# Hybrid encoder: a granule of the Fourier output weights split earlier, and a half tile's transposing DMA moved behind the next product

## The chip, the cores and the metric

The kernel runs on one core of one Trainium2 chip. The metric is the device time of the whole program in microseconds (us), as the median of several runs. Lower is better.

## The reference

Two layers of three residual steps each, and a final RMSNorm, on 512 tokens of 1024 channels in float32:

```python
x = x + 0.5 * swiglu(rms_norm(x, g1), w_in1, w_out1)          # d_ff 2816
z = rms_norm(x, gm) @ mix_w_in                                # q, k, v, u, two gates
y_na = neighbourhood_attention(q, k, v, rpb) @ w_na_out       # 8 heads of 64, 8x64 grid
y_f = fft2(u, axes=(tokens, channels of a group)).real @ w_f_out
x = x + (sigmoid(ga + b0) * y_na + sigmoid(gf + b1) * y_f) @ w_o
x = x + 0.5 * swiglu(rms_norm(x, g2), w_in2, w_out2)
```

## The kernel before

**Arithmetic.** Products are made of three passes of a 12-bit-rounded high part and the remainder: for every weight granule (128 partitions by 1024 columns, 512 KB) ScalarE writes the rounded high part `whi` (line 191) and VectorE the low part `wlo` (line 194), and TensorE runs high by high, high by low and low by high (lines 502 to 505 in the large products, 316 to 318 in the others). The large products are done by a seven-product Strassen scheme, in the order 1, 5, 6, 2, 7, 3, 4 in the feed-forward stages. TensorE gets its work in this order, block after block.

**The weight stream.** A list of items, one per granule, is written out ahead in the order of use. `next` hands the next granule out and first splits two more (`AHEAD = 2`); every split of the item with number p first loads items up to number p + 7 (`FETCH = 8`):

```python
def fetch(self, to):                       # line 280
    while self.loaded < min(to, n) and ...: self.items[self.loaded].load(); ...
def prep(self, to):                        # line 286
    while self.prepped < min(to, n) and ...:
        self.fetch(self.prepped + self.depth)
        self.items[self.prepped].prep(...)
```

A load is a plain DMA on SP's queue (line 148). For two of the four quadrants of a block's weights, c and d, a second DMA on GpSimd's queue (line 150) then adds a into c and c into d in SBUF; these are the accumulating loads. A `Raw` object has `t` set to None until its load is traced. The raw buffers are nine, so most loads on SP wait for the `wlo` of an older granule.

**Feed-forward stage** (`stage_ffn`, four times). Five blocks, of fourteen items each, two for each of the seven products; in three of the stages the first block (`first_block`) has 21 items and half a block more. Items 2 and 3 of a block are d, items 8 and 9 are c (the first granule of a block has number 0). At the end of a block the gated result of the second half of the tokens, `z2`, is put through `halves`: `apart` (line 342) splits its 32-bit words into 16-bit halves with two ScalarE copies into `zs` and lets a transposing DMA on SP's queue (line 348) write `zt`. Then comes product 4, the last of the block, and then the same for `z1`. In the next block ScalarE joins the halves again (`joined`, line 357, `at<-zt`). After the last block of a stage it joins z1 first.

ScalarE, VectorE and SP's queue are ordered by the scheduler here, which simulates the program and takes what is ready, lines higher up first. Instructions of one engine run in the order in which the scheduler put them.

**Mixer** (`stage_mixer`, twice). Here the order on ScalarE, VectorE and TensorE is the order of the code. The part around lines 1577 to 1611: the Fourier branch's low parts `yf` (line 1247), the scores of attention steps 2 and 3 (`p2`, `p3`: row maxima at line 1295, exponentials at 1304, reciprocals at 1307, scaling at 1312), the key projection `k3` on TensorE, then `rows_of(yf, 0, first_f)`, the Fourier branch's output product, which needs two weight granules. `ws.prep(ws.pos + 1)` at 1585 splits the first of them, `ws.prep(ws.pos + 2)` at 1593 the second.

Of the kernel before, what the change touches and what calls it, by code (L numbers as in the profile page):

```python
# [9 lines left out]
F32 = mybir.dt.float32  # L10
# [3 lines left out]
U16 = mybir.dt.uint16  # L14
# [4 lines left out]
P = 128  # L19
# [72 lines left out]
def encoder_kernel(  # L92
    ctx: ExitStack, tc: tile.TileContext, xin, xtr, wst, gains, gfin, gbias, bias_in, dft, chan, ident_in, rot, out
):
    nc = tc.nc
# [12 lines left out]
    def nm(s):  # L108
        uid[0] += 1
        return f"{s}_{uid[0]}"  # L110

    def slot(dt=F32, s="k", shape=(4, 256)):
        return kp.tile([P, *shape], dt, tag="k", name=nm(s), bufs=23)
# [38 lines left out]
    class Item:  # L152
# [26 lines left out]
        def prep(self, nxt):  # L179
# [16 lines left out]
                G.dma_start(out=t, in_=wst[GRAN_AT[self.then]][:, 0:n], accum_op=ALU.add)  # L196
            self.out = (hi, lo)

    def stage_items():
        items, st = [], 0  # L200

        def add(*a, **k):
            items.append(Item(*a, stage=st, **k))

        def strassen(s, name, idx, sizes, order, dma=False, behind=None):
            def key(q, g):
                return (s, name(q), idx, g) if g < 2 else (s, "h" + q, idx, 0)

            r = {}
            for q, q2 in (("a", None), ("b", None), ("c", "a"), ("d", "c")):  # L210
                r[q] = [Raw(key(q, g), n, q2 and key(q2, g)) for g, n in enumerate(sizes)]
            d2 = [Raw(key("d", g), n) for g, n in enumerate(sizes)]
            at = [(m, g) for m in order for g in range(len(sizes))]
            if len(sizes) == 3:
                at.remove((2, 2))
                at.insert(at.index((7, 2)), (2, 2))
            for m, g in at:
                a, b, c, d = [r[q][g] for q in "abcd"]
                if m == 1:
                    add(a, neg=True)  # L220
                elif m == 2:
                    add(b)
                elif m == 3:
                    add(d, None if dma else b)
                elif m == 4:
                    add(d2[g])
                elif m == 5:
                    add(d)
                elif m == 6:
                    add(d, a, then=b.key if dma else None)  # L230
                else:
                    add(c)
                for key in (behind or {}).get(m, ()) if g == len(sizes) - 1 else ():
                    add(Raw(key))

        def out_sizes(c):
            return (1024, 512) if c == 0 else (1024, 1024)

        def ffn(s):
            first = not items  # L240
            if first:
                for g in range(4):
                    add(Raw((s, "cl", g)), parts=2 if g < 2 else 1, pieces=2 if g == 0 else 1)
            for j in range(NB):
                order = (1, 2, 5, 6, 7, 3, 4) if first and j == 0 else (1, 5, 6, 2, 7, 3, 4)
                strassen(s, lambda q: q, j, (1024,) * (2 if first or j else 3), order)
            for order in ((1,), (2,), (5, 6, 7, 3), (4,)):
                for c in range(3):
                    summed = s == (L - 1, 2) and c == 2
                    strassen(s, lambda q: "o" + q, c, out_sizes(c), order, summed)  # L250

        for l in range(L):
            ffn((l, 1))
            st += 1
            s = (l, 0)
            two = (1024, 1024)
            qk = [(s, "qk", g) for g in range(8)]
            strassen(s, lambda q: "u" + q, 0, two, (1, 5, 6, 2, 3, 7, 4), True, behind={5: qk[0:1], 6: qk[1:2], 2: qk[2:3], 3: qk[3:4], 7: qk[4:5]})
            for key in qk[5:] + [(s, "f", g) for g in range(4)]:
                add(Raw(key))  # L260
            st += 1
            for g in range(2):
                add(Raw((s, "n", 0, g)))
            st += 1
            for i in range(2):
                strassen(s, lambda q: "g" + q, i, two, ORDER, True)
            for g in range(2):
                add(Raw((s, "n", 1, g)))
            strassen(s, lambda q: "w" + q, 0, two, ORDER, True)
            ffn((l, 2))  # L270
        return items
# [40 lines left out]
    ws = Stream()  # L312
# [26 lines left out]
            V.scalar_tensor_tensor(r, t, 1.5, r, ALU.add, ALU.mult)  # L339
        return r  # L340

    def apart(z):

        s, t = slot(U16, "zs", (2, 4, 2, P)), slot(U16, "zt", (2, 4, 256))
        words = z.bitcast(U16).rearrange("p b (q f h) -> p h q b f", q=4, h=2)
        for h in range(2):
            S.activation(s[:, h], words[:, h], AF.Copy)  # L347
        nc.sync.dma_start_transpose(
            out=t.rearrange("p h q (b t) -> p (h q b) t", b=2), in_=s.rearrange("p h q b f -> p (h q b f)")
        )  # L350
        return t

    def joined_words(to, t):

# [254 lines left out]
    def stage_ffn(norm, nxt, late):  # L609

        hx, lx = norm.h, norm.l
        at = {}

        def at_tile(h, j, c):
# [72 lines left out]
        def halves(z, j, f0):  # L687

            turned.append((apart(z), j, f0))

        def joined():

# [35 lines left out]
        def times(z, u, j):  # L728
            for b in range(2):
                c = 2 * j + b  # L730
                V.scalar_tensor_tensor(z[:, b, :], u[b], norm.r2[:, c : c + 1], z[:, b, :], ALU.mult, ALU.mult)  # L731
# [68 lines left out]
        def first_block():  # L800

            f0 = 2

            def snap_T(ps):
                t = slot(F32, "sn", (2, 256))
                S.activation(t, ps.rearrange("p (m t) -> p m t", m=2), AF.Copy)
                return t

            def less_T(ps, t):
                V.tensor_tensor(t, ps.rearrange("p (m t) -> p m t", m=2), t, ALU.subtract)  # L810

            pa, ha = pair("A"), bank("hA")
            product(pa, acts[1], K4, True)
            combine(5)
            s1 = snap(pa)
            if len(norm.due) == 2:
                norm.quad(*norm.due.pop(0))
            product_T(ha, acts[1], True)
            h1 = snap_T(ha)
            pb, hb = pair("B"), bank("hB")  # L820
            product(pb, acts[5], K4, True)
            combine(6)
            sb = snap(pb)
            norm.settle()
            product_T(hb, acts[5], True)
            hsb = snap_T(hb)
            norm.rstd()
            norm.spread(R)
            product(pa, acts[6], K4, False, again=True)
            s2 = snap(pa)  # L830
            combine(7)
            product_T(ha, acts[6], False)
            h2 = snap_T(ha)
            pc = pair("C")
            product(pc, acts[2], K4, True)
            less(pc, s1)
            combine(4)
            z1 = gate(s1, 0)
            product(pa, acts[7], K4, False, again=True)
            hc = bank("hC")  # L840
            product_T(hc, acts[2], True)
            less_T(hc, h1)
            r1 = half_gate(h1, 0)
            less(pa, sb)
            product_T(ha, acts[7], False)
            less_T(ha, hsb)
            product(pb, acts[3], K4, False, again=True)
            less(pb, s2)
            z2 = gate(s2, 1)
            times(z2, [sb[:, 0, :], sb[:, 1, :]], 1)  # L850
            product_T(hb, acts[3], False)
            less_T(hb, h2)
            r2 = half_gate(h2, 1)
            half_times(h2, r2, hsb, hsb, 1)
            halves(z2, 1, f0)
            product(pa, acts[4], K4, False, again=True)
            times(z1, pa, 0)
            halves(z1, 0, f0)
            product_T(ha, acts[4], False)
            half_times(h1, r1, ha.rearrange("p (m t) -> p m t", m=2), h2, 0)  # L860
# [4 lines left out]
        for jb in range(0 if first else 1, NB):  # L865
# [35 lines left out]
                make(1)  # L901
            z2 = gate(s2, 1)
            times(z2, [sb[:, 0, :], sb[:, 1, :]], 1)
            halves(z2, 1, f0)
            if jb == NB - 1:
                make(2)
            product(pa, acts[4], K4, False, again=True)
            times(z1, pa, 0)
            halves(z1, 0, f0)

# [137 lines left out]
    def stage_mixer(l, norm, nxt):  # L1048
# [427 lines left out]
        yf = []  # L1476
# [24 lines left out]
        with tc.manual_schedule(engines={mybir.EngineType.DVE, mybir.EngineType.Activation}):  # L1501
            with tc.manual_schedule(engines={mybir.EngineType.PE}):
# [77 lines left out]
                q3 = q3()  # L1580
                p2, p3 = [Probs(i, att_scores(i)) for i in (2, 3)]
                k3 = proj_T(None, 0)
                p2.maxes(0)
                p2.maxes(1)
                ws.prep(ws.pos + 1)
                p2.exps(0)
                p2.exps(1)
                p3.maxes(0)
                p2.inverse(0)
                p3.maxes(1)  # L1590
                p2.inverse(1)
                yf += [w0(), w1()]
                ws.prep(ws.pos + 2)
                p2.scaled(0)
                p2.scaled(1)
                p3.exps(0)
                k[2] = k2()
                p3.inverse(0)
                p3.exps(1)
# [394 lines left out]
```

## Time and profile before

| | |
|---|---|
| median of 3 runs | 1852.29 us (1851.4, 1852.29, 1854.55) |
| the profiled execution | 1856.7 us |
| its span, first to last instruction | 1854.9 us |
| busy in it: TensorE / VectorE / ScalarE / GpSimd | 1838.5 / 1601.6 / 1312.2 / 173.1 us |
| mean granted TensorE clock | 0.998 |
| mean DMA rate | 213 GB/s |

Rows of a timeline read: start in us, duration in us, engine, line, operation, tiles written <- read, shape, count of merged instructions, and in brackets the engine's idle time ahead of it and what ended it. PE is TensorE, DVE VectorE, ACT ScalarE, POOL GpSimd; SPq is SyncE, all of whose instructions issue DMAs: an instruction there lasts from its start on the queue, with its wait, until it has been issued.

### The profile page before, as it was taken

Reading aid. Unit: us, or ns where it says so; the run is one execution under the profiler, and the core shown is the slowest. Engines: PE = TensorE matmul, PEld = TensorE weight load, DVE = VectorE, ACT = ScalarE, POOL = GpSimd, SP = SyncE. Lnnn points to the kernel's source line nnn. Section 1 sums busy time; section 2 is a strip of 40 time slices with the busy share of each in tenths; the row PEclk is TensorE's granted clock in tenths of the full one; section 3 lists DMA queues with packets and bytes.
Section 4 is the critical chain, followed back from the end, with each engine's and each line's share of the span. In section 5 each row is a group of like instructions: output and inputs, shape, how many; then the busy total and the mean of one; then the engine's idle time right before and its main releaser. Section 6 shows DMA issues by size and latency. Waiting matters only on the chain.

```text
span 1854.9 us, 24564 instructions
## 1 busy us (share of the span) xinstructions
PE 1838.5 (99%) x8850; PEld 1530.0 (82%) x8850; DVE 1601.6 (86%) x1942; ACT 1312.2 (71%) x1777; POOL 173.1 (9%) x212
## 2 busy tenths in 40 slices
PE   9999999999999999999999999999999999999998
PEld 7888888888888888888888888888888888788886
DVE  7878899786989987889998888998869899787898
ACT  6777875668576777777667778665776776677865
POOL 0001010100111010001010100101001111010010
PEclk9999999999999999999999999999999999999999
DMA  9898799934887798979888887988258866989795
GB/s 297 229 231 223 189 275 272 232 103 126 236 234 173 180 221 228 211 198 270 248 197 225 222 218 198 284 288 187 85 181 201 227 174 184 201 225 218 214 282 148
DMA packets 198282, 395.72 MB, mean 213 GB/s; under 512 B 103760, under 2 KB 103888, under 8 KB 198160
## 3 DMA queue, kind: packets, MB, share of 16 engines
q1 hardware_dynamic: 168912, 294.23, 50.4%
q0 software_dynamic: 28816, 99.38, 30.2%
q8 instruction: 69, 1.13, 0.2%
q10 hardware_dynamic: 432, 0.55, 0.1%
q14 instruction: 53, 0.43, 0.1%
HBM read 367.88 MB, written 2.11 MB: 199 GB/s over the span
## 4 chain that ended last, share of the span: by engine, by line
PE 88%; DVE 4%; ACT 3%; DMA 2%; issue 1%; SPq 0%; ACTq 0%; DVEq 0%
PE A L505 9%; PE A L502 9%; PE A L503 9%; PE o L505 7%; PE o L502 7%; PE o L503 7%; PE B L503 5%; PE B L502 5%; PE B L505 5%; PE C L502 2%; PE C L503 2%; PE C L505 2%; PE ps L316 2%; PE ps L317 2%; PE ps L318 2%; DMA zt<-zs 2%
## 5 line engine op out<-in xcount | busy, mean ns | idle before, releaser
L194 DVE TENSOR_TENSOR wlo<-raw,whi 128x1024 fp32r<-128x1024 f32 (+1 forms) x534 | 630.0, 1189 | 183.9 <-ACT whi L191 180.0
L191 ACT ACTIVATE whi<-raw 128x1024 fp32r<-128x1024 f32 (+1 forms) x534 | 545.4, 1033 | 253.4 <-DVE raw L164 53.2
L150 POOL DMA_DIRECT2D raw<-in_wst_dram x166 | 144.3, 889 | 1361.0 <-DMA raw<-in_wst_dram 532.1
L164 DVE TENSOR_TENSOR raw<-raw,raw 128x1024 f32<-128x1024 f32 (+1 forms) x148 | 175.9, 1189 | 2.0
L503 PE MATMUL A<-whi,xl 128*128 128x512 f32 x400 | 155.7, 389 | 0.0
L502 PE MATMUL A<-whi,xh 128*128 128x512 f32 x400 | 155.7, 389 | 0.0
L357 ACT ACTIVATE at<-zt 128x1024 uint16<-128x1024 uint16 (+2 forms) x96 | 110.2, 1166 | 22.9 <-DMA zt<-zs 22.9
L186 ACT ACTIVATE whi<-raw 128x1024 fp32r<-128x1024 f32 (+1 forms) x83 | 85.9, 1037 | 44.0 <-issue 12.5
L505 PE MATMUL A<-wlo,xh 128*128 128x512 f32 x400 | 115.0, 389 | 0.0
L187 DVE SCALAR_TENSOR_TENSOR wlo<-raw,whi 128x1024 fp32r<-128x1024 f32 (+1 forms) x83 | 98.2, 1191 | 12.7 <-ACT whi L186 12.7
L505 PEld LDWEIGHTS A<-wlo,xh 128*128 128x128 f32 x400 | 75.1, 188 | 15.5
L503 PEld LDWEIGHTS A<-whi,xl 128*128 128x128 f32 x400 | 75.1, 188 | 15.4
L502 PEld LDWEIGHTS A<-whi,xh 128*128 128x128 f32 x400 | 75.1, 188 | 15.4
L502 PE MATMUL C<-whi,xh 128*128 128x512 f32 x208 | 81.1, 390 | 0.1
L503 PE MATMUL C<-whi,xl 128*128 128x512 f32 x208 | 81.0, 389 | 0.0
L502 PE MATMUL B<-whi,xh 128*128 128x512 f32 x208 | 81.0, 389 | 0.0
L503 PE MATMUL B<-whi,xl 128*128 128x512 f32 x208 | 81.0, 389 | 0.0
L724 ACT ACTIVATE th<-sn,rh 128x512 f32<-128x512 f32 x80 | 55.1, 716 | 36.1 <-DVE sn L577 35.2
L347 ACT ACTIVATE zs<-th 128x1024 uint16<-128x1024 uint16 x80 | 79.5, 1042 | 1.3 <-DVE th L731 1.3
L572 ACT ACTIVATE sn<-A 128x512 f32<-128x512 f32 x104 | 59.0, 583 | 23.6 <-PE A L505 23.6
L505 PE MATMUL C<-wlo,xh 128*128 128x512 f32 x208 | 59.8, 389 | 0.0
L505 PE MATMUL B<-wlo,xh 128*128 128x512 f32 x208 | 59.8, 389 | 0.0
(428 smaller groups left out, 4678.8 us busy)
## 6 DMA issues: line engine op xcount, KB each, us to landing
raw<-in_wst_dram SPq DMA_DIRECT2D x468, 512.0 KB, 5.9
raw<-in_wst_dram POOLq DMA_DIRECT2D x176, 512.0 KB, 7.9
bm<-in_bias_dram SPq DMA_DIRECT2D x16, 512.0 KB, 4.4
raw<-in_wst_dram SPq DMA_DIRECT2D x30, 256.0 KB, 4.5
x<-in_xin_dram SPq DMA_DIRECT2D x4, 512.0 KB, 10.2
raw<-in_wst_dram POOLq DMA_DIRECT2D x8, 256.0 KB, 8.6
dft<-in_dft_dram POOLq DMA_DIRECT2D x8, 256.0 KB, 11.0
gb<-in_gbias_dram SPq DMA_DIRECT2D x4, 512.0 KB, 9.1
```

The costliest lines, as they stand in the source:

```text
L150: G.dma_start(out=self.t, in_=wst[GRAN_AT[self.plus]][:, 0 : self.n], accum_op=ALU.add)
L164: V.tensor_tensor(self.raw.t, self.raw.t, self.add.t, ALU.add)
L186: S.activation(hi, t, AF.Copy, scale=-1.0)
L187: self.last = V.scalar_tensor_tensor(lo, t, -1.0, hi.bitcast(F32), ALU.mult, ALU.subtract)
L191: S.activation(hi[:, cs], t[:, cs], AF.Copy)
L194: self.last = V.tensor_tensor(lo[:, cs], t[:, cs], hi[:, cs].bitcast(F32), ALU.subtract)
L347: S.activation(s[:, h], words[:, h], AF.Copy)
L357: S.activation(to[:, w], t[:, w], AF.Copy)
L502: PE.matmul(ps, lh, rh, start=start, stop=False, skip_group_check=again)
L503: PE.matmul(ps, ll, rh, start=False, stop=False, skip_group_check=again)
L505: PE.matmul(ps, lh, rl, start=False, stop=stop, skip_group_check=again)
L572: S.activation(t[:, b, :], ps[b], AF.Copy)
```

## The change

Two edits.

In the mixer, the four VectorE instructions of `w0()` and `w1()` go ahead of p2's maxima; the second granule's high part (ScalarE) goes ahead of p2's exponentials, its low part (VectorE) behind p2's reciprocals; and the second pair of p3's maxima goes behind the granule's low part and behind p3's first exponentials.

In the feed-forward stages, `apart` is cut in two. The ScalarE copies of z2 stay where they were. Its transposing DMA is written behind product 4, inside `behind_sums`: where the accumulating load of granule 1 of quadrant c of the next block has been traced, a DMA of 64 bytes out of that granule's buffer is issued on SP, and the transposing DMA is queued behind it; where that load has not been traced (`raw.t is None`) or there is no next block, nothing is added.

```diff
@@ strassen
+                sums.update({z.key: z for z in r[q] if z.plus})
@@ apart
-    def apart(z):
-        s, t = slot(U16, "zs", (2, 4, 2, P)), slot(U16, "zt", (2, 4, 256))
+    def words_apart(z):
+        s = slot(U16, "zs", (2, 4, 2, P))
...
+    def turned_words(s):
+        t = slot(U16, "zt", (2, 4, 256))
         nc.sync.dma_start_transpose(
...
+    def apart(z):
+        return turned_words(words_apart(z))
@@ stage_ffn
+        stage = (norm.idx // 3, 1 + (norm.idx % 3) // 2)
...
+        def behind_sums(jb):
+            raw = sums.get((stage, "c", jb, 1))
+            if raw is None or raw.t is None:
+                return nullcontext()
+            seen = dp.tile([16], F32, tag="seen", name=nm("seen"))
+            to = bass.AP(tensor=seen.tensor, offset=seen.offset, ap=[[16, 1], [1, 16]])
+            return tc.issue_after(nc.sync.dma_start(out=to, in_=raw.t[0:1, 0:16]))
@@ first_block (the other blocks alike, with jb + 1)
-            halves(z2, 1, f0)
+            z2 = words_apart(z2)
             product(pa, acts[4], K4, False, again=True)
+            with behind_sums(1):
+                turned.append((turned_words(z2), 1, f0))
             times(z1, pa, 0)
             halves(z1, 0, f0)
@@ stage_mixer
                 k3 = proj_T(None, 0)
+                yf += [w0(), w1()]
                 p2.maxes(0)
                 p2.maxes(1)
                 ws.prep(ws.pos + 1)
+                low = ws.prep_high()
                 p2.exps(0)
                 p2.exps(1)
+                p2.inverse(0)
                 p3.maxes(0)
-                p2.inverse(0)
-                p3.maxes(1)
                 p2.inverse(1)
-                yf += [w0(), w1()]
-                ws.prep(ws.pos + 2)
+                low()
                 p2.scaled(0)
                 p2.scaled(1)
                 p3.exps(0)
+                p3.maxes(1)
                 k[2] = k2()
```

More of the change, by code (lines that the diff above doesn't have):

```diff
@@ L197, in prep @@
             self.out = (hi, lo)
+    sums = {}
     def stage_items():
@@ L347, in apart @@
             S.activation(s[:, h], words[:, h], AF.Copy)
+        return s
+    def turned_words(s):
+        t = slot(U16, "zt", (2, 4, 256))
         nc.sync.dma_start_transpose(
@@ L903, in stage_ffn @@
             times(z2, [sb[:, 0, :], sb[:, 1, :]], 1)
-            halves(z2, 1, f0)
+            z2 = words_apart(z2)
             if jb == NB - 1:
@@ L907, in stage_ffn @@
             product(pa, acts[4], K4, False, again=True)
+            with behind_sums(jb + 1):
+                turned.append((turned_words(z2), 1, f0))
             times(z1, pa, 0)
```

## The prediction

> **What bounds the kernel now.** I read the page first, then what TensorE waits for, then the timelines around the two waits that the edits touch.
>
> ```profile
> span 1854.9 us, 24564 instructions
> PE 1838.5 (99%) x8850; PEld 1530.0 (82%) x8850; DVE 1601.6 (86%) x1942; ACT 1312.2 (71%) x1777; POOL 173.1 (9%) x212
> PE 88%; DVE 4%; ACT 3%; DMA 2%; issue 1%; SPq 0%; ACTq 0%; DVEq 0%
> ```
>
> TensorE is busy for all but 1854.9 − 1838.5 = 16.4 us, the start and the end of the program included. Neither edit removes a matmul, so a gain can only come out of these 16 us. The view of TensorE's own waits names two that matter inside the program:
>
> ```profile
> PE A L502 <- ACT whi L191: 2.7, 1, 2.7
> PE ps L317 <- DVE wlo L194: 2.1, 2, 1.0
> ```
>
> The second is the Fourier output product waiting for its second weight granule, once in each mixer; the first edit is about it. The first is one long wait, in which a transposing DMA has a part; the second edit bears on that. A time within 0.2% of 1852.29 us, that is within 3.7 us, is about what a measurement of this kernel can tell from no change.
>
> **The mixer edit.** TensorE's timeline in the two mixers:
>
> ```profile
> 425.00 0.39 PE L317 MATMUL ps<-wlo,y 128*128 128x512 f32 x1
> ...
> 425.91 0.39 PE L318 MATMUL ps<-whi,y 128*128 128x512 f32 x1
> 426.14 0.39 PE L316 MATMUL ps<-whi,y 128*128 128x512 f32 x1
> 427.56 0.50 PE L317 MATMUL ps<-wlo,y 128*128 128x512 f32 x1 [1.04 <-DVE wlo L194]
> ...
> 1344.28 0.39 PE L316 MATMUL ps<-whi,y 128*128 128x512 f32 x1
> 1345.69 0.50 PE L317 MATMUL ps<-wlo,y 128*128 128x512 f32 x1 [1.03 <-DVE wlo L194]
> ```
>
> Matmuls of this shape start 426.14 − 425.91 = 0.23 us apart. The step at the wait is 427.56 − 426.14 = 1.42 us in the first mixer and 1345.69 − 1344.28 = 1.41 in the second, so each wait costs 1.42 − 0.23 = 1.19 us and the two together 2.4 us. That is all there is to gain here. Whether it is gained depends on when VectorE ends the low part in the new order. The old order:
>
> ```profile
> 419.46 0.41 DVE L1295 CUSTOM_DVE_ANT_0 s<-ps,bm 128x256 f32<-128x256 f32 x1
> ...
> 421.52 1.23 DVE L194 TENSOR_TENSOR wlo<-raw,whi 128x1024 fp32r<-128x1024 f32 x1 [0.60 <-ACT whi L191]
> 422.66 0.42 DVE L1295 CUSTOM_DVE_ANT_0 s<-ps,bm 128x256 f32<-128x256 f32 x1
> ...
> 423.35 0.16 DVE L1307 RECIPROCAL rs<-sm 128x2 f32<-128x2 f32 x1
> 423.42 0.40 DVE L1295 CUSTOM_DVE_ANT_0 s<-ps,bm 128x256 f32<-128x256 f32 x1
> ...
> 424.17 2.20 DVE L1247 TENSOR_TENSOR y<-fy,y 128x256 fp32r<-128x256 f32 x4
> 426.30 1.21 DVE L194 TENSOR_TENSOR wlo<-raw,whi 128x1024 fp32r<-128x1024 f32 x1
> ```
>
> From start to start, the four low parts y take 426.30 − 424.17 = 2.13 us, a pair of maxima 423.35 − 422.66 = 0.69, a reciprocal 0.07, a granule's low part 422.66 − 421.52 = 1.14. In the new order the y go first: 419.46 to 421.59. Two pairs of p2's maxima: to 422.97. First granule's low part: to 424.11, complete 1.23 after its start, at 424.20; TensorE wants it at 425.00, so this delay of 1.45 us is covered with 0.8 us to spare. Reciprocal, one pair of p3's maxima, reciprocal: 0.83, to 424.94. Second granule's low part: complete 1.21 later, at 426.15. TensorE heard of the old one 427.56 − (426.30 + 1.21) = 0.05 after its end, so here at 426.20, and wants it at 426.14 + 0.23 = 426.37. The wait goes, with 0.17 us to spare. ScalarE must not be later than that:
>
> ```profile
> 420.41 1.07 ACT L191 ACTIVATE whi<-raw 128x1024 fp32r<-128x1024 f32 x1
> 421.36 0.52 ACT L1304 ACTIVATE s<-s,nmx 128x256 f32<-128x256 f32 x1
> ...
> 423.33 1.06 ACT L191 ACTIVATE whi<-raw 128x1024 fp32r<-128x1024 f32 x1
> 424.28 1.71 ACT L1312 ACTIVATE s<-s,rs 128x256 f32<-128x256 f32 x4
> ```
>
> The second high part moves to 421.36 and takes 0.95, so p2's exponentials run from 422.31 for 423.33 − 421.36 = 1.97 us, to 424.28. Their first maxima are there at 422.3, the second reciprocal asks for the last sum at 424.87, 0.6 us after it is written, and the scaling starts at 424.28 as before. The moved pair of p3's maxima ends at about 424.94 + 1.14 + 0.69 = 426.8, when the exponentials that need it are due on ScalarE. No load moves with the granule: the Fourier granules are the last of the stream's stage, and all four are fetched before this point. TensorE then runs 1.19 us earlier into products that follow it one for one. The gain is between 0 (the low part 1.2 us later than worked out, all spare time wrong) and 2.4 us for both mixers; I take 2.4, since every term has its own row and the sum leaves something over.
>
> **The transposing DMA.** The first question is whether the tiny transfer is issued at all. The lookup wants granule 1 of quadrant c of the next block, item 9 of that block. Product 4 takes the last two items of a block. The last `next` splits item 1 of the next block, and that split has loaded items up to 1 + 7 = 8, which is granule 0 of c. In the first block of 21 items one more granule of the block is still to come, and the loads reach item 7. So at each of the 20 places `raw.t` is None or there is no next block, and nothing is added: no transfer, no wait, no forced order. I cost it at nothing; nobody queues behind it.
>
> What is left is that the transposing DMA of z2 is written behind product 4 rather than ahead of it, so behind the two granule loads that this product issues on SP. GpSimd's queue holds none of the moved work; its accumulating load for granule 0 of c still waits for the plain load. Does the DMA's place on SP's queue change? SP's order is not the code's:
>
> ```profile
> 986.31 7.92 SPq L348 DMA_TRANSPOSE zt<-zs  x2
> 994.33 5.46 SPq L148 DMA_DIRECT2D raw<-in_wst_dram  x3
> ```
>
> This is a first block: both transposing DMAs, z2's and z1's, stand ahead of the loads, though z1's is written behind product 4's two loads even now. The loads have no free buffer at that time, and the scheduler takes what is ready. With z2's DMA written just ahead of z1's, it is ready as early as before and the loads no earlier, so I expect the same order there and in the other blocks, and a cost between −1 and +1 us; I take 0.
>
> That leaves the long wait, in the first block of the last stage:
>
> ```profile
> 1582.82 0.86 POOL L150 DMA_DIRECT2D raw<-in_wst_dram  x1 [10.35 <-DMA raw<-in_wst_dram]
> 1583.97 0.85 POOL L150 DMA_DIRECT2D raw<-in_wst_dram  x1 [0.29 <-DVE at L798]
> ...
> 1584.03 19.88 SPq L348 DMA_TRANSPOSE zt<-zs  x2
> ...
> DMA to landing us min/median/max: 4.3/5.7/20.2
> ...
> 1604.29 1.36 ACT L357 ACTIVATE at<-zt 128x1024 uint16<-128x1024 uint16 x1 [4.92 <-DMA zt<-zs]
> ...
> 1608.27 0.50 PE L502 MATMUL A<-whi,t7h 128*128 128x512 f32 x1 [2.73 <-ACT whi L191]
> 1613.18 0.39 PE L502 MATMUL A<-whi,t7h 128*128 128x512 f32 x1
> ...
> 1608.50:1613.50 5.00, 5.00 (x16) 3.91 (x16) 5.00 (x6) 3.87 (x5) 0.81 (x1) 0.66 0.98 364
> ```
>
> An accumulating load was issued 0.06 us before the transposing DMA started. The two then held each other up: 20.2 us to landing against a median of 5.7. ScalarE stood still for 4.92 us before `at<-zt`, the weight split behind it was late, and TensorE waited 2.73 us. The 14 matmul steps from 1608.27 to 1613.18 then took 4.91 us instead of 14 × 0.23 = 3.2, at a granted clock of 0.66. The event cost 2.7 + 1.7 = 4.4 us. It is one of three such first blocks; the other two show nothing on TensorE. The accumulating load in it is the one for d of the next block, not the c that the edit names.
>
> The Trainium skill, DMA: Bandwidth & Descriptors, Rules for kernel authors, says that a transpose next to ordinary DMAs needs nothing; the 20.2 us row speaks against that as far as time goes, if an accumulating load counts as ordinary, and by the rule no reordering on SP could win anything. TensorE: Matmul & The Clock Gate, What's actually happening, has the clock fall after an idle window of about 3.4 us; here it fell after 2.73, and by the rule the event would have cost 2.7 us, not 4.4.
>
> **The sum.** The profiled execution took 1856.7 us, 1.8 more than its span. Less the 2.4 of the mixers it gives 1854.3 if the long wait comes again. The median of the runs, 1852.29, is 4.4 under the profiled one, just what the long wait cost, so I read the median as a time without it: 1852.29 − 2.4 = 1849.9 us, 0.13% faster.
>
> **Rivals.**
>
> Forecast, chance 0.46: the mixers' waits go, SP's order stays, 1849.9. Its own range is 1848.3 to 1852, from the gain's end at zero and from the runs' distance from their median; 0.10 of the 0.46 lies under 1848.6.
>
> The transposing DMA comes free of the accumulating load, 0.24. Written later, z2's DMA goes out some us after the load that it met, and the long wait is absent from the timed runs. For it: the event hangs on 0.06 us, and the slowest of the three runs is 2.3 above the median, so part of it may be in them. Against: nothing forces the order. Full price 1852.29 − 2.4 − 4.4 = 1845.5.
>
> The mixer edit brings nothing, 0.10: the low part meets a wait that the sum does not show (a maximum waiting for TensorE, a late exponential), eating the 0.17 us to spare and 1.2 more. 1852.3, within 0.2%.
>
> Slower, 0.20: SP does follow the code. In the last block of each stage z1 is joined first, and its DMA lands just in time:
>
> ```profile
> 821.03 3.54 SPq L348 DMA_TRANSPOSE zt<-zs  x1
> 824.67 1.01 SPq L148 DMA_DIRECT2D raw<-in_wst_dram  x2
> 827.03 2.90 SPq L348 DMA_TRANSPOSE zt<-zs  x1
> ...
> 833.76 2.58 ACT L357 ACTIVATE at<-zt 128x1024 uint16<-128x1024 uint16 x2 [3.60 <-DMA zt<-zs]
> ```
>
> With the two loads ahead, z2's DMA would start at 824.67 + 1.01 = 825.7 and hold SP for 3.54, to 829.2, so z1's starts 2.2 us later than at 827.03. ScalarE is already standing there, so TensorE pays most of 2.2, in four stages 8.8: 1852.29 − 2.4 + 8.8 = 1858.7. It decides from the point where z2's DMA stands behind both loads there. Against: the first-block rows. I put 0.16 over 1856.0 and 0.04 under.
>
> **How the numbers follow.** Faster by over 0.2%: 0.10 + 0.24 = 0.34. Within: 0.36 + 0.10 + 0.04 = 0.50. Slower: 0.16. The range leaves out the slower case's upper part and little else: from the second case's full price, 1845.5, to 1854.5, the profiled sum with the long wait in it.
>
> **What would show it.** Right: no wait of line 317 for `wlo` in either mixer, and the second granule's low part about 0.2 us ahead of its matmul; 44 transposing DMAs and no new small transfer on SP; z2's DMA ahead of product 4's loads as now. Wrong: a tiny transfer on SP, or loads ahead of z2's DMA with z1's later by 2 us in the last blocks; a new TensorE wait in the mixers; more than one transposing DMA over 10 us.

## The result and the profile after

| | before | after |
|---|---|---|
| median | 1852.3 us (16 runs, 1850.31 to 1854.55) | 1848.24 us (16 runs, 1846.36 to 1850.91) |
| ratio, 95% interval | | 0.9978 [0.9971, 0.9984] |
| profiled execution / its span | 1856.7 / 1854.9 us | 1848.85 / 1847.1 us |

The changed kernel is 1852.3 − 1848.24 = 4.06 us or 0.22% faster; the forecast was 1849.9 us, 2.4 us faster, with a range of 1845.5 to 1854.5. The two profiled executions differ by more, 7.85 us, because the one before held the long wait of 4.4 us.

The head of the page after:

```profile
span 1847.1 us, 24562 instructions
PE 1835.1 (99%) x8850; PEld 1528.9 (83%) x8850; DVE 1602.5 (87%) x1942; ACT 1312.4 (71%) x1777; POOL 173.1 (9%) x212
```

TensorE's idle time has shrunk from 16.4 us to 1847.1 − 1835.1 = 12.0, with as many matmuls. TensorE's own waits (total us, times, longest us):

```profile
PE ps L136 <- DVE ones L132: 1.2, 1, 1.2
PE cl L514 <- ACT whi L191: 0.8, 1, 0.8
PE o L517 <- DVE wlo L194: 0.7, 1, 0.7
PE cl L515 <- DVE xl L329: 0.3, 1, 0.3
PE cl L517 <- DVE wlo L194: 0.2, 1, 0.2
```

Both waits on which the prediction rested are gone: `ps` for `wlo` in the mixers, and the long one of `A`. The mixer lines have moved: the products that stood at 316 to 318 are at 319 to 321, the low part of the moved granule at 175. VectorE's timeline in the first mixer, and TensorE's beside it:

```profile
419.08 4.33 DVE L1273 TENSOR_TENSOR y<-fy,y 128x256 fp32r<-128x256 f32 x8
...
424.70 1.22 DVE L194 TENSOR_TENSOR wlo<-raw,whi 128x1024 fp32r<-128x1024 f32 x1
425.83 0.16 DVE L1333 RECIPROCAL rs<-sm 128x2 f32<-128x2 f32 x1
...
426.66 1.20 DVE L175 TENSOR_TENSOR wlo<-raw,whi 128x1024 fp32r<-128x1024 f32 x1
```

```profile
427.63 0.39 PE L321 MATMUL ps<-whi,y 128*128 128x512 f32 x1
427.85 0.40 PE L319 MATMUL ps<-whi,y 128*128 128x512 f32 x1
428.09 0.39 PE L320 MATMUL ps<-wlo,y 128*128 128x512 f32 x1
```

The matmul with the second granule's low part (428.09) follows the one before it without a gap. The low part ends at 426.66 + 1.20 = 427.86; with the 0.05 us that TensorE took to hear of it in the kernel before that is 427.91, and it is wanted at 427.85 + 0.23 = 428.08: 0.17 us to spare.

The feed-forward edit did move something. SyncE's queue and ScalarE in the last block of the second stage, the place for which the prediction showed 821.03 to 827.03 and the wait of 3.60 us:

```profile
821.34 5.29 SPq L356 DMA_TRANSPOSE zt<-zs  x2
826.72 5.67 SPq L148 DMA_DIRECT2D raw<-in_wst_dram  x5
...
822.81 1.99 ACT L350 ACTIVATE zs<-th 128x1024 uint16<-128x1024 uint16 x2
824.70 2.00 ACT L186 ACTIVATE whi<-raw 128x1024 fp32r<-128x1024 f32 x2
...
830.33 2.58 ACT L369 ACTIVATE at<-zt 128x1024 uint16<-128x1024 uint16 x2
```

The two transposing DMAs now stand one behind the other, ahead of the loads, so z1's goes out earlier rather than later, and the join `at<-zt` starts at 830.33 with no wait where it started at 833.76 after one of 3.60. ScalarE's copies of z1 (822.81) have come ahead of two granule splits (824.70). Laid side by side, instruction by instruction on each engine, the two programs differ in the feed-forward stages only here: SyncE's queue has a new order in the four last blocks and nowhere else; ScalarE and VectorE have one in the same four places and, behind the last block of the second stage alone, in its output products too. TensorE's and GpSimd's orders are the same throughout. No instruction writes `seen`: the tiny transfer was issued nowhere.

The view by tile, transposing DMAs: the time from issue to landing, and below it how long one held SyncE's queue (minimum, median and maximum in ns, then the first and the last start in us):

```profile
DMA to landing us min/median/max: 4.3/5.6/10.4
L356 SPq DMA_TRANSPOSE zt<-zs x44: 1356/3568/7882, 72.6 to 1740.0; - x44
```

The longest now lands after 10.4 us, not 20.2.

### The profile page after: what moved, and what is told of

Read it like the earlier page. It is cut to its first block, busy times and chain, and to the rows that moved or that the text cites. A ratio compares the mean times of both kernels' runs of the same rounds, so it can differ in the third digit from the quotient of the medians.

```text
span 1847.1 us, 24562 instructions
## 1 busy us (share of the span) xinstructions
PE 1835.1 (99%) x8850; PEld 1528.9 (83%) x8850; DVE 1602.5 (87%) x1942; ACT 1312.4 (71%) x1777; POOL 173.1 (9%) x212
## 4 chain that ended last, share of the span: by engine, by line
PE 91%; DVE 4%; DMA 2%; issue 2%; ACT 1%; POOL 0%; SPq 0%; DVEq 0%; ACTq 0%; POOLq 0%
PE A L514 10%; PE A L517 10%; PE A L515 10%; PE o L517 5%; PE o L514 5%; PE o L515 5%; PE B L515 5%; PE B L514 5%; PE B L517 5%; PE ps L319 4%; PE ps L320 3%; PE ps L321 3%; PE C L515 3%; PE C L517 3%; PE C L514 3%
```

## The experiments

The theory (A) was two separate gains: 2.4 to 2.7 us from the mixers and 1.2 to 1.6 from the last blocks. The rivals were that the mixer edit does it all (B), that the feed-forward edit frees the transposing DMA from the accumulating loads and would win more if the tiny transfer were really issued (C), and that the tiny transfer makes late what is queued behind it (D). The four kernels that follow ran on one chip, with 29 runs of the kernel before, median 1851.65 us.

**e1_mixer: the mixer edit alone.** The mixer hunk of the change, nothing else.

```diff
                 k3 = proj_T(None, 0)
+                yf += [w0(), w1()]
...
+                low = ws.prep_high()
                 p2.exps(0)
...
-                yf += [w0(), w1()]
-                ws.prep(ws.pos + 2)
+                low()
...
                 p3.exps(0)
+                p3.maxes(1)
```

> The kernel before with the mixer edit alone. Theory A (two separate gains): the two Fourier waits go and nothing else, -2.4 to -2.7 us, about 1849.7; in the profile the transposing DMA of z1 in the last block of a stage is issued behind two loads as before, and ScalarE waits for it there. Rival B (the mixer edit does it all, the rest by a different timing of the first blocks behind the mixers): -4 us, 1848.3.

Measured: 1848.97 us (1847.02 to 1851.15, 11 runs), ratio 0.9988 [0.9979, 0.9996], 2.7 us faster by the medians. TensorE's waits:

```profile
PE ps L136 <- DVE ones L132: 1.2, 1, 1.2
PE cl L505 <- DVE wlo L194: 0.3, 1, 0.3
PE cl L502 <- ACT whi L191: 0.2, 1, 0.2
```

No `ps` waits for `wlo`. Most of the 4.06 us is the mixers'. The time alone does not exclude rival B: its 1848.3 us would be a ratio of 0.9982, inside the interval.

**e2_last and e10_last: z2's transposing DMA moved in the last block of each stage only.** The mixers are as before. The kernel ran twice, the second time (e10_last) on another chip with 23 runs of the kernel before, median 1851.41 us.

```diff
-            halves(z2, 1, f0)
-            if jb == NB - 1:
+            if jb < NB - 1:
+                halves(z2, 1, f0)
+            else:
+                z2 = words_apart(z2)
                 make(2)
             product(pa, acts[4], K4, False, again=True)
+            if jb == NB - 1:
+                turned.append((turned_words(z2), 1, f0))
```

> The kernel before with the transposing DMA of z2 moved in the last block of each stage only; the mixers are as before. Theory A: -1.2 to -1.6 us, about 1850.9, because z1's DMA goes out 2 to 4 us earlier there and ScalarE no longer waits for it. Rival B: within 0.3 us of before. Rival C (fewer clashes of a transposing DMA with an accumulating load in the first blocks are the rest): within 0.3 us of before, since the first blocks are not touched.

> The last-block edit alone a second time, for its size. From the profiles: the second stage's out products lose about 1 us of waiting, the other stages nothing: -0.6 to -1.2 us against the kernel before. If the first measurement was right: -0.3 or less.

Measured: 1851.26 us, ratio 0.9997 [0.9988, 1.0005], and 1850.53 us, ratio 0.9994 [0.9986, 1.0003], 11 runs each; by the medians 0.4 and 0.9 us faster. Neither interval excludes no change, and both medians fall short of the 1.2 to 1.6 us that theory A gave the first time; the second is inside the 0.6 to 1.2 expected of it. What the profiles add is a place. In the output products of the second stage, behind its last block, VectorE is further ahead. Before, on VectorE and TensorE:

```profile
905.18 1.21 DVE L194 TENSOR_TENSOR wlo<-raw,whi 128x1024 fp32r<-128x1024 f32 x1
...
906.45 1.20 PE L505 MATMUL o<-wlo,c3h 128*128 128x512 f32 x4 [0.45 <-DVE wlo L194]
```

and the same low part in e2_last:

```profile
902.28 1.21 DVE L194 TENSOR_TENSOR wlo<-raw,whi 128x1024 fp32r<-128x1024 f32 x1
```

It comes 2.90 us earlier, and TensorE's wait is gone. (0.53 of the 2.90 us had been won ahead of this stretch: the matmul at 860.14 us before stands at 859.61 in e2_last.) Taken over that stretch, from the same matmul at 860 us to the same at 930 us, and counted from the shortest of all profiles, the kernels with the old order in the last block took 1.32 (before), 0.75 (e1), 1.11 (e5), 1.43 (e6) and 2.05 us (e8), 1.33 on average; those with the new one 0 (after, e2, e3, e7, e9, e10) and 1.03 (e4), 0.15 on average. So about 1.2 us come from there by the profiles, 0.4 to 0.9 by the two comparisons; e4, the changed kernel once more, shows that not every execution has the gain.

**e4_after: the changed kernel again**, on the chip of e1 to e3.

> The changed kernel once more, on the same chip as the three others. Both theories: -4.0 us, 1848.3. Theory A: the sum of the mixer edit alone and the last-block edit alone, within 0.5 us.

Measured: 1848.08 us (11 runs), ratio 0.9981 [0.9972, 0.9989], 3.6 us faster. The mixers' 2.7 and the last blocks' 0.4 to 0.9 make 3.1 to 3.6; with the 4.06 of the first comparison that leaves 0.5 to 1 us, which is inside the intervals and has no place in a profile.

**e3_tiny: the tiny transfer really issued.** The mixers are as before; z2's DMA is moved as in the change, but the lookup asks for quadrant d, whose accumulating load has been traced by then, so that 16 tiny transfers go out. The order of everything else, on every engine, is that of e2_last.

```diff
-            raw = sums.get((stage, "c", jb, 1))
+            raw = sums.get((stage, "d", jb, 1))
...
-            return tc.issue_after(nc.sync.dma_start(out=to, in_=raw.t[0:1, 0:16]))
+            return tc.issue_after(nc.sync.dma_start(out=to, in_=raw.t[0:1, 0:16]).ins)
```

> The kernel before with the transposing DMAs moved in all blocks, the mixers as before, and the lookup changed from quadrant c to quadrant d, whose accumulating load has been traced by then: sixteen tiny transfers are issued, each waiting for that load, with the transposing DMA and what stands behind it on SP queued behind. Theory A: the wait only takes the place of one that the transposing DMA had anyway while the accumulating load was in flight, no transposing DMA takes over 10 us, and the time is that of the last-block edit alone, 1850.9, within 0.7. Rival C: clashes cost a part of the median, so it is 1 us or more faster than the last-block edit. Rival D (what is queued behind the tiny transfer is late): over 1853.5.

Measured: 1882.57 us (1863.44 to 1902.1, 6 runs), ratio 1.0138 [1.0105, 1.017]: 31 us slower by the medians, 26 by the ratio. This is rival D by its size. SyncE's waits for the transfer, TensorE's, and ScalarE's for the transposed words:

```profile
SPq L711 <- DMA raw<-in_wst_dram: 136.2, 16, 9.9
...
PE A L514 <- ACT whi L191: 18.4, 4, 8.2
...
ACT at L369 <- DMA zt<-zs: 50.4, 13, 11.8
```

TensorE's waits for weight splits come to 18.4 us here and 3.3 in two smaller groups. The mean granted clock of this execution is 0.993 where the others without tiny transfers have 0.998 or 0.999; I put the rest of the 31 us down to that, without having worked it out.

One block of it, on SyncE's queue and GpSimd:

```profile
749.09 0.25 SPq L711 DMA_DIRECT2D seen<-raw  x1
749.42 0.80 SPq L148 DMA_DIRECT2D raw<-in_wst_dram  x2
752.14 5.92 SPq L356 DMA_TRANSPOSE zt<-zs  x1
...
758.80 10.85 SPq L356 DMA_TRANSPOSE zt<-zs  x1
...
753.61 0.86 POOL L150 DMA_DIRECT2D raw<-in_wst_dram  x1 [3.32 <-DMA raw<-in_wst_dram]
```

The tiny transfer waits for the accumulating load of d. The plain loads queued behind it, granule 1 of c among them, go out only at 749.42; c's accumulating load, which needs that plain load, follows at 753.61 and is in flight with z2's transposing DMA (752.14) and z1's (758.80, which holds the queue for 10.85 us). In the kernel before, the same place of the same block has the last of c's accumulating loads 2.44 us ahead of z2's transposing DMA, and each transposing DMA holds the queue for 3.4 us:

```profile
742.14 0.86 POOL L150 DMA_DIRECT2D raw<-in_wst_dram  x1 [4.49 <-DMA raw<-in_wst_dram]
...
744.58 3.38 SPq L348 DMA_TRANSPOSE zt<-zs  x1
...
748.69 3.41 SPq L348 DMA_TRANSPOSE zt<-zs  x1
```

Two causes remain: the wait on SyncE's queue itself, 136 us of it, or the meeting that it brings about.

**e7_tiny_no_c and e8_no_c: without c's accumulating loads.** e7 is e3 with them left out in the feed-forward blocks, e8 is the kernel before with them left out; c is then used without a added, so that the two compute something else and serve for their times alone. These two and the two that follow ran on one chip with 19 runs of the kernel before, median 1851.38 us.

```diff
             for q, q2 in (("a", None), ("b", None), ("c", "a"), ("d", "c")):
+                if q == "c" and name("c") == "c":
+                    q2 = None
```

> The kernel with the sixteen tiny transfers, with the accumulating loads of quadrant c in the feed-forward blocks left out (c is used without a added; the loads for d stay). Theory K (the 31 us of the tiny transfers come from transposing DMAs that are delayed into the accumulating load of c and hold each other up): most of it goes, 1851 to 1858. Rival W (they come from SP's queue standing still behind the tiny transfer, the weight loads late): 1875 or more, as with c's loads.

> The kernel before with the accumulating loads of quadrant c in the feed-forward blocks left out, nothing else: the reference time for the run with tiny transfers and without c's loads. TensorE's work is the same: 1850 to 1852.5, at most 2 us faster than before if these loads cost anything there.

Measured: e7 1850.87 us, ratio 0.9996 [0.9986, 1.0005]; e8 1850.64 us, ratio 0.9997 [0.9988, 1.0006]; 10 runs each. Waits in e7 of SyncE, of TensorE and of ScalarE for the transposed words, and its transposing DMAs:

```profile
SPq L713 <- DMA raw<-in_wst_dram: 123.2, 16, 9.7
...
PE ps L322 <- DVE wlo L194: 2.1, 2, 1.0
...
ACT at L371 <- DMA zt<-zs: 8.7, 4, 2.3
...
L358 SPq DMA_TRANSPOSE zt<-zs x44: 1338/2880/4077, 72.6 to 1740.6; - x44
```

The 16 waits of up to 9.7 us are all still on SyncE's queue, and they cost nothing that these runs can tell. Without c's accumulating loads no transposing DMA holds the queue for more than 4.1 us, and the 31 us are gone. ScalarE's waits for the transposed words are 8.7 us against 50.4 in e3, while its waits for loaded weights (`whi` for the DMA of `raw`) are much the same, 20.4 and 23.0: it was the transposing DMAs that came late, not c's weights. So the loss of e3 is the meeting. e8 shows that taking these loads out gains 0.7 us in itself by the medians and 2.2 at most by the interval, so it does not hide a loss of that size in e7.

**e5_high and e6_maxes: the mixer edit taken apart.** e5 forms the granule's high part ahead of p2's exponentials and leaves VectorE's order alone. e6 is e1 with the second pair of p3's maxima kept ahead of the low part. One run each.

```diff
 e5
                 ws.prep(ws.pos + 1)
+                low = ws.prep_high()
...
-                ws.prep(ws.pos + 2)
+                low()
 e6, against e1
                 p2.inverse(1)
+                p3.maxes(1)
                 low()
...
                 p3.exps(0)
-                p3.maxes(1)
```

> The kernel before, in the mixers the second granule's high part alone formed ahead of p2's exponentials; VectorE's order is as before, its low part behind the four y. Theory V (VectorE's order makes the wait): TensorE still waits for wlo once in each mixer, as long as before or up to 0.3 us longer, since p2's exponentials and with them the second reciprocal come 0.95 us later; the view of TensorE's waits shows 1.0 to 1.3 for each. Rival S (the high part was the late one): the waits are gone.

> The kernel before with the mixer edit, except that the second pair of p3's maxima stays ahead of the second granule's low part. Theory V with the prediction's terms: the low part is 0.69 us later, the spare 0.17 us is used up, and TensorE waits 0.52 us in each mixer beyond its usual step (0.3 to 0.5 in the view of its waits, which counted 1.04 for 1.19 before). If the spare were larger than worked out: no wait, or a smaller one.

Measured: e5 1851.35 us, e6 1849.97 us; for runs taken once the waits are the measure. In e5, TensorE, and on VectorE the low part:

```profile
PE ps L317 <- DVE wlo L175: 2.7, 2, 1.4
...
426.22 1.21 DVE L175 TENSOR_TENSOR wlo<-raw,whi 128x1024 fp32r<-128x1024 f32 x1
```

The high part is ready earlier, but the low part starts at 426.22, as before the change (426.30), since it stands behind the same y, and the waits stay. VectorE's order is what counts. In e6:

```profile
PE ps L317 <- DVE wlo L175: 0.8, 2, 0.4
...
425.80 0.39 PE L316 MATMUL ps<-whi,y 128*128 128x512 f32 x1
426.58 0.50 PE L317 MATMUL ps<-wlo,y 128*128 128x512 f32 x1 [0.39 <-DVE wlo L175]
```

The step at the wait is 426.58 − 425.80 = 0.78 us, 0.55 more than a matmul's 0.23. The prediction's rows give 0.69 for the pair of maxima less 0.17 to spare, 0.52. So VectorE's order and the place of the maxima are both needed, and the sums hold to a few hundredths of a us. VectorE's new order with the high part left where it was has not been run; whether that piece is needed stays open.

**e9_first: the change with three tiny transfers**, in the three first blocks only; the order of everything else is that of the changed kernel. It ran with e10_last.

```diff
-            raw = sums.get((stage, "c", jb, 1))
+            raw = sums.get((stage, "d", jb, 1))
... in the other blocks:
-            with behind_sums(jb + 1):
+            with nullcontext():
                 turned.append((turned_words(z2), 1, f0))
```

> The changed kernel with three tiny transfers, one in each first block, where the lookup is changed to quadrant d; in all other blocks none. It differs from the changed kernel in these three instructions on SP alone. If a clash of a transposing DMA with d's accumulating load in a first block is rare (one in the profiles so far), the wait neither gains nor costs in the median: 1847.4 to 1848.9 where the changed kernel takes 1848.1. If such clashes cost a part of the median: below 1847. If the wait delays the transposing DMA into c's accumulating load there as well: over 1850.

Measured: 1853.31 us (1847.63 to 1866.61, 12 runs), ratio 1.001 [0.9997, 1.0022] to the kernel before, some 5 us above the changed kernel. I had expected no change in the median; what came is the last case of the expectation, "over 1850". In its profile TensorE waits for a weight split in the first blocks of the second and the last stage:

```profile
PE A L514 <- ACT whi L191: 11.6, 2, 6.8
```

SyncE's transposing DMAs and GpSimd's accumulating loads of c in the first block of the last stage (4.8 of the 11.6 us), and under them the same in the third stage, where nothing waits:

```profile
1588.98 0.86 POOL L150 DMA_DIRECT2D raw<-in_wst_dram  x1 [13.19 <-DVE at L820]
1590.56 0.85 POOL L150 DMA_DIRECT2D raw<-in_wst_dram  x1 [0.73 <-issue]
1589.88 21.81 SPq L356 DMA_TRANSPOSE zt<-zs  x2
...
992.24 0.85 POOL L150 DMA_DIRECT2D raw<-in_wst_dram  x1 [0.43 <-issue]
993.20 7.54 SPq L356 DMA_TRANSPOSE zt<-zs  x2
```

The changed kernel in the first block of the last stage:

```profile
1578.60 0.85 POOL L150 DMA_DIRECT2D raw<-in_wst_dram  x1 [0.31 <-issue]
1580.95 10.69 SPq L356 DMA_TRANSPOSE zt<-zs  x2
```

In a first block the tiny transfer is queued ahead of three plain loads, two of them c's, and these stand ahead of the transposing DMAs. So it does not part c's accumulating loads from the transposing DMAs; it delays them towards these. Where the last accumulating load went out 0.68 us behind the start of the first transposing DMA (1590.56 and 1589.88), the two transposes held the queue for 21.81 us; where it went out 0.96 us ahead (992.24 and 993.20), for 7.54. The first block of the second stage, with the other 6.8 us of the wait, is like the last stage's: the load went out 0.28 us behind (664.48 and 664.20), and the two held the queue for 24.74 us.

## Why the prediction was right, and where it was not

**How close it was.** The forecast gave 0.50 to a time within 0.2% of the kernel before and 0.34 to a time faster than that; what came, 0.22% faster, is the second. 1848.24 us lies just under the range of the forecast's own case, 1848.3 to 1852. It lies inside the stated range, which is 9 us wide because it reaches to the full price of a rival that did not come to pass; to that extent the hit was luck.

**The mixer step held, and its size was a little small.** The second granule's low part has the 0.17 us to spare that the sum gave, to the hundredth, as the rows after show. The size was 1.19 us for each wait. The stretch around it is 1.33 us longer before than after in the first mixer and 1.30 in the second, 2.6 for the two, and e1_mixer measures 2.7. Most of the missing 0.14 us is in the matmul behind the wait. Before:

```profile
427.56 0.50 PE L317 MATMUL ps<-wlo,y 128*128 128x512 f32 x1 [1.04 <-DVE wlo L194]
427.90 0.40 PE L318 MATMUL ps<-whi,y 128*128 128x512 f32 x1
```

The step behind it is 0.34 us, not 0.23, which is 0.11 of it. I had measured the step into the wait and not the one out of it.

**The tiny transfer** is absent, as the prediction worked out from the stream's positions. That cost term was right at zero.

**The step that failed** is the one on the transposing DMA: "so I expect the same order there and in the other blocks, and a cost between −1 and +1 us; I take 0." In 16 of the 20 blocks the order is the same. In the last blocks it is not, and the gain there is the part of the result that the forecast lacked: 0.4 to 0.9 us by the medians and 1.2 by the profiles, though no comparison of times excludes zero for it alone. Its reason was wrong too. I read the first block's rows as both transposing DMAs standing ahead of the loads that are written before z1's. By the tiles' names in the program the loads written ahead of them stand ahead of them; the three in the quoted row are later ones. What moves the DMA in a last block is its place behind `make(2)`, which the other blocks don't have; the likely reason is that the buffer of `zt` is now asked for behind those that `make(2)` asks for. A program with z2's DMA written just behind `make(2)`, still ahead of product 4, has the same order as the changed kernel. In all four last blocks `zt` and the tile that `make(2)` writes have other buffers than before, and in two of them the tile has the one that was `zt`'s. All this is read off programs; that one was not run, and how the scheduler gets from the buffers to z1's DMA was not followed.

**The rival "slower"** named that place and wait, but had its direction wrong: z1's DMA goes out ahead of two loads, not behind them. The 3.60 us that ScalarE won there did not come through to TensorE as such. What did come is the earlier low part in the output products. It comes just where, in this stage alone, ScalarE and VectorE have a new order in the output products as well. How the earlier DMA leads to that order was not followed, so that link is argued and not shown.

**The long wait.** The sum took the median before as free of it, and subtracted nothing. That holds as far as the runs tell: of the profiles of kernels without tiny transfers, that of the kernel before alone has it, and the changed kernel gained 3.6 to 4.1 us with 3.1 to 3.6 accounted for. So the rival "clash freed" did not come to pass at its price of 4.4 us; whether it takes part in the last few tenths stays open. One sentence about it was wrong: the accumulating loads that met the transposing DMA (1582.82 and 1583.97) are the two granules of c of the next block, those that the edit names. Tracing had just not reached granule 1 of c where the lookup asks for it.

**The two rules.** The Trainium skill, DMA: Bandwidth & Descriptors, Rules for kernel authors, holds that a transpose next to ordinary DMAs needs nothing. The sentence stands there in a row on transposes that corrupt each other and does not speak of time, so "no reordering on SP could win anything" did not follow from it. e3_tiny and e7_tiny_no_c show that next to accumulating loads a transpose can cost 31 us in a program of 1851. On the clock, TensorE had a granted clock under 1 beside each of its waits of 2.73 us and more within the program (2.73 before, 2.74, 4.97 and 8.16 in e3_tiny, 4.78 and 6.83 in e9_first), and of 1.00 beside one of 2.50 in e3_tiny. The Trainium skill (TensorE: Matmul & The Clock Gate, What's actually happening) has the clock fall after an idle window of about 3.4 us. The 2.73 and 2.74 us, as the profile counts a wait, lie under that; no run here was aimed at the length at which the clock falls.

## What to carry to other kernels

When a wait is to be removed by reordering, list every instruction between the operand and its use from start to start, also the small ones: here a spare of 0.17 us came out to the hundredth, and one pair of maxima left in the way brought 0.55 us of wait back. Moving a line past something that asks for buffers changed a queue's order here, where moving it past a product did not, so look for what else asks for buffers between the old place and the new. And a wait put on a queue to keep two transfers apart also delays the loads queued behind it: look whether the transfer that it should avoid is one of those that these loads release.

## What the runs showed of the hardware

When an accumulating load is issued at about the time at which a transposing DMA starts, both can take much longer. In the kernel before one such transposing DMA took 20.2 us to land against a median of 5.7, and in e9_first one took 19.6:

```profile
DMA to landing us min/median/max: 4.4/5.5/19.6
```

When 16 waits made them meet more often, the time rose from 1851.65 to 1882.57 us and the runs spread over 39 us; without c's accumulating loads it was 1850.87, with the same waits.

The moment of issue separates the two cases cleanly. In the twelve profiles 494 accumulating loads were issued within 10 us of the start of a transposing DMA. Ten of them took 12.1 to 24.6 us to land, and they are the ten that were issued between 0.06 us ahead of that start and 1.47 us behind it: one in the kernel before, two in e9_first, seven in e3_tiny. The other 484 were issued 0.15 us or more ahead, or 1.82 us or more behind, and took 11.4 us at most. The accumulating loads have this row in the view of DMA issues before (count, KB each, median us to landing):

```profile
raw<-in_wst_dram POOLq DMA_DIRECT2D x176, 512.0 KB, 7.9
```

At 7.9 us each, those issued 0.15 to a few us ahead were in flight with the transposing DMA as well. So it is not the overlap alone that counts, but the moment at which the accumulating load is issued. Why it decides was not tried.
